# Products of the identity set between a mixer's narrow products, and one run of narrow products cut in two

## The chip, the core and the metric

The kernel runs on one core of one Trainium2 chip. The metric is the device time of one launch, in microseconds (us). Three runs of the kernel before took 1149.23, 1156.27 and 1161.38 us; their median is 1156.27 us.

## What is computed

Two layers, each on 256 tokens of width 1024, then one last RMS norm. A layer is a SwiGLU feed-forward block, a mixer, and a second feed-forward block, each added to the residual with a gate, each on an RMS norm that is scaled and shifted by nine vectors from a conditioning vector. The mixer projects its input once and feeds three branches:

- attention: an indexer of 8 heads of 32 scores every key for every query, the 64 best keys of a query are kept, and 8 heads of 64 attend to these alone (one key and value head is shared by all);
- a state-space mixer: 16 groups of 16 channels with a complex state of 64, written here in chunks of 8 tokens (32 chunks), so that the input of a group's state is one product with a 128 x 128 matrix `R`;
- a convolution of 31 taps with a layer norm and a product.

The three are normalised, joined, and multiplied by `w_out`. All is float32. In the wide products a float32 operand is split into a high and a low part (`hi`, `lo`), and three products of these (helper `mm3`, lines 328 to 330) give the result.

## The kernel before, in words

**Tiling.** Tokens are two tiles of 128 (`t` = 0, 1). The weights come from HBM in units of 128 x 1024, in the order in which they are used; `Stream.prep_one` (lines 100 and 102) splits each unit on ScalarE and VectorE. The feed-forward blocks and the mixer's projections and `w_out` are made of wide products: a moving operand of 256 to 512 columns against 128 rows.

**The mixer** (`mixer`) has eight generators: `W` the projection (one step is 24 wide products, tiles `ps_inB`, `ps_inQ`), `K` the keys, `I` and `J` the indexer for tile 0 and 1 (`att_index`, tile `ps_idx`, line 1201), `S` the state-space branch (`ssm_thread`), `C` the convolution, `a` and `b` the attention for tile 0 and 1 (`att_main`). A string, `MIX_ORDER`, lists whose step is traced next. Around the change it reads `... I W I S J S I W I J J I S W ...`; the third `S` is the run of 16 products `R` x `U` into `ps_V` (line 1301), each 32 columns wide, then two copies to ScalarE's tile `Vs` (1303, 1304).

**The narrow products.** An indexer step makes two products of 32 rows and 128 columns (tile 0) or 256 columns (tile 1). In `att_main`, tile 0 has two banks of four heads and tile 1 four banks of two heads; each head has three products into `ps_lg`: the mask in bfloat16 through the identity `identb` (line 1247), then the high and the low part of the keys (1249, 1250), 128 or 256 columns wide. Then the probabilities are transposed, four 128-column transposes to a bank `ps_PT` (1265), two banks for tile 0 and four for tile 1, and multiplied with the values, 64 columns wide, into `ps_o` (1270).

**What sets the order.** Each engine works its queue in order. The order in a queue is made when the kernel is built: the framework's planner plays the program on a timeline of its own and takes, of the instructions that are ready there, the one traced first. `tc.issue_after(x)` puts the instructions of its block behind `x` on `x`'s engine, with no wait. So a product traced early can come late in the queue, and products of different steps are mixed.

**PSUM.** `ps_idx`, `ps_lg` and `ps_PT` take the banks `a2` and `a3` in turn (two of the `ps_lg` take another pool), `ps_U`, `ps_V` and `ps_Y` the bank `a0`. A product with `start=True` begins its columns anew: what stood there is gone.

Of the kernel before, what the change touches and what calls it, by code (L numbers as in the profile page):

```python
# [17 lines left out]
P = 128  # L18
# [21 lines left out]
NCH = 32  # L40
# [3 lines left out]


MIX_ORDER = """
W K S K K W K J I J J I W I S J S I W I J J I S W I J I J S W C C C I J J I S W
I J I J S I J S W W C C S W a b S N a C a C S S b b a C a b C b a a b b b C b b
b
"""  # L50
# [81 lines left out]
def kernel(  # L132
# [8 lines left out]
    nc = tc.nc  # L141
# [19 lines left out]
    def s1(shape, dtype, nm, tg="a"):  # L161
        return two_p.tile(shape, dtype, tag="s1" + tg, name=nm, bufs=S1B[tg])

    def s2(shape, nm, tg="a", dtype=F32):
        return two_p.tile(shape, dtype, tag="s2" + tg, name=nm, bufs=S2B[tg])

    def b8(shape, nm):
        return two_p.tile(shape, F32, tag="b8", name=nm, bufs=2)

    def bank(pool, nm):  # L170
        return pool.tile([P, 512], F32, tag="b", name=nm)

    def abank(i, nm):
        return ps_a.tile([P, 512], F32, tag=f"a{i}", name=nm)


    ident = const.tile([P, P], F32, name="ident")
    make_identity(nc, ident)
    identb = const.tile([P, P], BF16, name="identb")
    nc.gpsimd.tensor_copy(identb, ident)  # L180
    ones = const.tile([P, 32], F32, name="ones")
    nc.gpsimd.memset(ones, 1.0)
    dmask = ident[:, 112:128]
# [911 lines left out]
    def mixer(l, finish):  # L1095
# [7 lines left out]
        kTl = one_p.tile([P, 256], F32R, tag="kTl", name="kTl")  # L1103
        kiT = one_p.tile([P, 256], F32, tag="kiT", name="kiT")
        qiT = s2([P, 512], "qiT")
# [8 lines left out]
        def merge(t, piece, k0, nk):  # L1114

            pt = bank(ps_m, "ps_mg")
            for k in range(nk):
                nc.tensor.transpose(pt[:, P * k:P * k + P], piece[:, P * k:P * k + P], ident)
            for k in range(nk):
                merged(t, k0 + k, pt[:, P * k:P * k + P], xTh[t][:, k0 + k, :], xTl[t][:, k0 + k, :])  # L1120
# [73 lines left out]
        def att_index(t):  # L1194
            nk = P * (t + 1)
            idx = s1([P, 256], F32, "idx")
            for b in range(4):

                ps = abank(2 + b % 2, "ps_idx")
                for i in range(2):  # L1200
                    nc.tensor.matmul(ps[:, nk * i:nk * i + nk], qiT[32 * b:32 * b + 32, 256 * i + P * t:256 * i + P * t + P],  # L1201
                                     kiT[32 * b:32 * b + 32, :nk], start=True, stop=True)
                rl = s2([P, 512], "rl")
                nc.scalar.activation(rl[:, :2 * nk], ps[:, :2 * nk], AF.Relu, scale=32 ** -0.5)
                for i in range(2):
                    h = b + 4 * i
                    if h == 0:
                        nc.vector.tensor_scalar_mul(idx[:, :nk], rl[:, :nk], wis[:, t, 0:1])
                    else:
                        nc.vector.scalar_tensor_tensor(idx[:, :nk], rl[:, nk * i:nk * i + nk], wis[:, t, h:h + 1],  # L1210
                                                       idx[:, :nk], op0=ALU.mult, op1=ALU.add)
                yield
            nc.vector.memset(idx[0:64, nk - 64:nk], NEG_INADM)
            for r in range(8):
                m8 = sm_p.tile([P, 8], F32, tag="m8", name="m8")
                nc.vector.max(m8, idx[:, :nk])
                nc.vector.match_replace(idx[:, :nk], m8, idx[:, :nk], NEG_TAKEN)
                yield
            mb = s1([P, 256], BF16, "maskb")
            nc.vector.tensor_scalar(mb[:, :nk], idx[:, :nk], NEG_CUT, MASK_BIAS, op0=ALU.is_gt, op1=ALU.mult)  # L1220
            maskb[t] = mb
            yield

        def att_main(t):
            nk = P * (t + 1)
            hpb = 512 // nk
            nb = 8 // hpb

            qT = [s2([P, 512], f"qT{e}", "a", F32R) for e in range(2)]
            for j in range(2):  # L1230
                src = pin["Q"][j].rearrange("p (k n) -> p k n", k=2)[:, :, P * t:P * t + P]
                for e in range(2):
                    r, o = slice(64 * e, 64 * e + 64), slice(64 - 64 * e, P - 64 * e)
                    d = qT[e].rearrange("p (k j n) -> p k j n", k=2, j=2)[:, :, j]
                    nc.scalar.activation(d[r], src[r], AF.Copy)
                    nc.vector.tensor_sub(d[o], src[r], d[r].bitcast(F32))
            yield
            Pm = b8([P, 8, 256], "Pm")
            sums = sm_p.tile([P, 8], F32, tag="sums", name="sums")
            mx = sm_p.tile([P, 8], F32, tag="mx", name="mx")  # L1240
            nmx = sm_p.tile([P, 8], F32, tag="nmx", name="nmx")
            for b in range(nb):
                ps = bank(ps_g, "ps_lg") if t == 1 and b < 2 else abank(2 + b % 2, "ps_lg")
                hb = [2 * (hpb * (b // 2) + i) + b % 2 for i in range(hpb)]
                for i, h in enumerate(hb):
                    r = 64 * (h % 2)
                    nc.tensor.matmul(ps[:, nk * i:nk * i + nk], identb, maskb[t][:, :nk], start=True, stop=False)
                    qh = qT[h % 2][:, P * (h // 2):P * (h // 2) + P]
                    nc.tensor.matmul(ps[:, nk * i:nk * i + nk], qh, kTh[:, :nk], start=False, stop=False)
                    nc.tensor.matmul(ps[:, nk * i:nk * i + nk], qh[r:r + 64], kTl[r:r + 64, :nk], start=False, stop=True)  # L1250
                hs = slice(hb[0], hb[-1] + 1, 2)
                nc.vector.tensor_reduce(mx[:, hs], ps.rearrange("p (h n) -> p h n", h=hpb), axis=mybir.AxisListType.X, op=ALU.max)
                nc.vector.tensor_scalar_mul(nmx[:, hs], mx[:, hs], -0.125)
                for i, h in enumerate(hb):
                    nc.scalar.activation(Pm[:, h, :nk], ps[:, nk * i:nk * i + nk], AF.Exp, bias=nmx[:, h:h + 1],
                                         scale=0.125, accum_out=sums[:, h:h + 1])
                yield
            rin = sm_p.tile([P, 8], F32, tag="rin", name="rin")
            nc.vector.reciprocal(rin, sums)
            po = bank(ps_g, "ps_o")  # L1260
            for b in range(nb):
                pt = abank(2 + b % 2, "ps_PT")
                for i in range(4):
                    h, kt = (4 * b + i, 0) if t == 0 else (2 * b + i // 2, i % 2)
                    nc.tensor.transpose(pt[:, P * i:P * i + P], Pm[:, h, P * kt:P * kt + P], ident)
                PT = s2([P, 512], "PT")
                nc.scalar.activation(PT, pt, AF.Copy)
                for i in range(4):
                    h, kt = (4 * b + i, 0) if t == 0 else (2 * b + i // 2, i % 2)
                    nc.tensor.matmul(po[:, 64 * h:64 * h + 64], PT[:, P * i:P * i + P], vsb[:, kt, :],  # L1270
                                     start=(kt == 0), stop=(kt == t))
                yield
            o = s2([P, 512], "osb")
            nc.vector.tensor_mul(o.rearrange("p (h n) -> p h n", h=8), po.rearrange("p (h n) -> p h n", h=8),
                                 rin.rearrange("p (h o) -> p h o", o=1).to_broadcast([P, 8, 64]))
            rs = rms_col([o], 512)
            nc.vector.tensor_scalar_mul(o, o, rs)
            yield
            merge(t, o, 0, 4)
            yield  # L1280

        def ssm_thread():
            R, O, Tp, Ec, Es, D8 = (SS[n] for n in ("R", "O", "Tp", "Ec", "Es", "D8"))
# [9 lines left out]
            ps = abank(0, "ps_U")  # L1293
            for g in range(G):
                nc.tensor.transpose(ps[:, NCH * g:NCH * g + NCH], Ug[:, g].rearrange("c a j -> c (a j)"), ident[32:32 + NCH, 32:32 + NCH])
            U = s2([P, G, NCH], "U", "s")
            nc.scalar.activation(U.rearrange("p g n -> p (g n)"), ps, AF.Copy)
            yield
            psv = abank(0, "ps_V")
            for g in range(G):  # L1300
                nc.tensor.matmul(psv[:, NCH * g:NCH * g + NCH], R[:, g, :], U[:, g, :], start=True, stop=True)
            Vs = s2([P, 512], "Vs", "s")
            nc.scalar.activation(Vs[0:64, :], psv[64:128, :], AF.Copy)
            nc.scalar.activation(Vs[64:128, :], psv[0:64, :], AF.Copy)
# [23 lines left out]
            for g4 in range(4):  # L1328
                for gq in range(4):
                    g = 4 * gq + g4  # L1330
                    o_ = py[32 * gq:32 * gq + 32, P * g4:P * g4 + P]
                    nc.tensor.matmul(o_, U[:, g, :], Tp[:, :, g, :], start=True, stop=False, tile_position=(0, 32 * gq))
                for gq in range(4):
                    g = 4 * gq + g4
# [17 lines left out]
            pt = bank(ps_m, "ps_yT")  # L1352
# [8 lines left out]
            for q in range(4):  # L1361
                w_ = wg[q // 2]
                cs = slice(512 * (q % 2), 512 * (q % 2) + 512)
                for e in range(2):
                    r, qs = slice(64 * e, 64 * e + 64), slice(P * q, P * q + P)
# [15 lines left out]
            pt = bank(ps_m, "ps_sg")  # L1381
# [200 lines left out]
```

## Time and profile before

| | us |
|---|---|
| profiled execution, its own time | 1159.37 |
| its span on the core | 1157.5 |
| median of the three runs | 1156.27 |
| TensorE busy | 1082.1 (93%) |
| VectorE busy | 881.8 (76%) |
| ScalarE busy | 557.9 (48%) |
| mean granted TensorE clock | 0.954 of full |

The span goes from the first to the last instruction; the profiled execution took 1.9 us more than that. PE is TensorE's matmuls, PEld its weight loads, DVE VectorE, ACT ScalarE, POOL GpSimd, SP the queue of most loads. The granted clock of a stretch is 1.00 at 2.4 GHz and 0.50 at 1.2 GHz. Busy time of PE counts an instruction from its start to its modelled end, so two products in a row overlap in it; the distance from one start to the next is what one costs. In the trace a float32 product that is not split stands as two matmuls.

### The profile page before, as it was taken

Reading aid. Unit: us, or ns where it says so; the run is one execution under the profiler, and the core shown is the slowest. Engines: PE = TensorE matmul, PEld = TensorE weight load, DVE = VectorE, ACT = ScalarE, POOL = GpSimd, SP = SyncE. Lnnn points to the kernel's source line nnn. Section 1 sums busy time; section 2 is a strip of 40 time slices with the busy share of each in tenths; the row PEclk is TensorE's granted clock in tenths of the full one; section 3 lists DMA queues with packets and bytes.
Section 4 is the critical chain, followed back from the end, with each engine's and each line's share of the span. In section 5 each row is a group of like instructions: output and inputs, shape, how many; then the busy total and the mean of one; then the engine's idle time right before and its main releaser. Section 6 shows DMA issues by size and latency. Waiting matters only on the chain.

```text
span 1157.5 us, 19306 instructions
## 1 busy us (share of the span) xinstructions
PE 1082.1 (93%) x7043; PEld 936.8 (81%) x7043; DVE 881.8 (76%) x1791; ACT 557.9 (48%) x979; POOL 93.2 (8%) x176
## 2 busy tenths in 40 slices
PE   5999978998999999999998999999899998999996
PEld 3578867886886878888996799999698687999996
DVE  4479998888597687899856889889678777665655
ACT  4354433446436565563534534444464656444442
POOL 6000101021012000000020000100100000000000
PEclk9899999989797899999999999999999899999998
DMA  9889788996653139768873799999665234767651
GB/s 254 268 268 304 227 258 287 328 292 175 159 149 78 57 103 301 246 223 287 262 220 108 250 323 360 339 317 328 184 165 148 73 91 146 256 210 221 210 160 55
DMA packets 182671, 251.43 MB, mean 217 GB/s; under 512 B 20023, under 2 KB 132865, under 8 KB 182577
## 3 DMA queue, kind: packets, MB, share of 16 engines
q1 hardware_dynamic: 173728, 240.56, 65.3%
q0 software_dynamic: 5792, 7.52, 2.8%
q10 hardware_dynamic: 3056, 2.13, 0.9%
q8 instruction: 55, 0.90, 0.3%
q14 instruction: 40, 0.32, 0.1%
HBM read 245.19 MB, written 1.11 MB: 213 GB/s over the span
## 4 chain that ended last, share of the span: by engine, by line
PE 56%; DMA 7%; DVE 6%; ACT 3%; issue 2%; SPq 1%; ACTq 0%; DVEq 0%
PE ps_gt L328 7%; PE ps_gt L329 7%; PE ps_gt L330 7%; PE ps_y L330 5%; PE ps_y L328 5%; PE ps_y L329 5%; DMA raw<-in_mod_w_dram 3%; DMA raw<-in_ffn_w_gu_dram 2%; DVE lo L102 2%; DVE macc L365 2%; ACT hi L100 1%; PE ps_idx L1201 1%; PE ps_gu L328 1%; PE ps_gu L330 1%; PE ps_cv L1408 1%
## 5 line engine op out<-in xcount | busy, mean ns | idle before, releaser
L100 ACT ACTIVATE hi<-raw 128x1024 fp32r<-128x1024 f32 (+1 forms) x314 | 328.0, 1054 | 315.0 <-DMA raw<-in_ffn_w_gu_dram 105.5
L102 DVE TENSOR_TENSOR lo<-raw,hi 128x1024 fp32r<-128x1024 f32 (+1 forms) x314 | 379.1, 1214 | 121.6 <-ACT hi L100 117.6
L328 PE MATMUL ps_gt<-xTh,hi 128*128 128x256 f32 x1120 | 320.2, 288 | 10.4 <-DVE h L745 6.6
L330 PE MATMUL ps_gt<-xTh,lo 128*128 128x256 f32 x1120 | 314.8, 285 | 4.4 <-DVE lo L102 4.4
L329 PE MATMUL ps_gt<-xTl,hi 128*128 128x256 f32 x1120 | 317.7, 285 | 0.0
L328 PEld LDWEIGHTS ps_gt<-xTh,hi 128*128 128x128 f32 x1120 | 216.2, 193 | 17.4 <-DVE h L745 7.6
L330 PEld LDWEIGHTS ps_gt<-xTh,lo 128*128 128x128 f32 x1120 | 214.4, 193 | 6.2 <-DVE lo L102 5.7
L329 PEld LDWEIGHTS ps_gt<-xTl,hi 128*128 128x128 f32 x1120 | 216.7, 193 | 1.8 <-issue 0.8
L365 DVE SCALAR_TENSOR_TENSOR macc<-raw,cond,macc 128x512 f32<-128x512 f32 x224 | 166.3, 749 | 25.8 <-DMA raw<-in_mod_w_dram 24.3
L329 PE MATMUL ps_y<-lo,hTh 128*128 128x512 f32 x352 | 139.9, 397 | 1.5 <-DVE lo L102 1.5
L330 PE MATMUL ps_y<-hi,hTl 128*128 128x512 f32 x352 | 139.5, 396 | 1.0 <-DVE hTl L749 1.0
L328 PE MATMUL ps_y<-hi,hTh 128*128 128x512 f32 x352 | 133.6, 396 | 4.9 <-ACT hi L100 4.5
L397 POOL DMA_DIRECT2D spill<-mrow x64 | 31.3, 496 | 642.0 <-ACT mrow L394 640.5
L328 PEld LDWEIGHTS ps_y<-hi,hTh 128*128 128x128 f32 x352 | 66.0, 189 | 19.3 <-ACT hi L100 5.3
L330 PEld LDWEIGHTS ps_y<-hi,hTl 128*128 128x128 f32 x352 | 67.1, 191 | 17.1 <-DVE hTl L749 2.1
L329 PEld LDWEIGHTS ps_y<-lo,hTh 128*128 128x128 f32 x352 | 67.3, 191 | 16.3 <-DVE lo L102 3.6
L328 PE MATMUL ps_gu<-hi,xTh 128*128 128x512 f32 x96 | 39.8, 415 | 6.8 <-DVE xTh L324 6.8
L743 ACT ACTIVATE silu<-ps_gt 128x256 f32<-128x256 f32 x70 | 25.3, 378 | 40.8 <-PE ps_gt L330 40.7
L330 PE MATMUL ps_gu<-hi,xTl 128*128 128x512 f32 x96 | 39.7, 414 | 3.0 <-DVE xTl L325 3.0
L329 PE MATMUL ps_gu<-lo,xTh 128*128 128x512 f32 x96 | 38.6, 402 | 0.0
L745 DVE TENSOR_TENSOR h<-silu,ps_gt 128x256 f32<-128x256 f32 x70 | 28.0, 417 | 10.6 <-ACT silu L743 10.4
L748 ACT ACTIVATE hTh<-h 128x256 fp32r<-128x256 f32 x70 | 27.4, 410 | 16.6 <-DVE h L745 15.5
(386 smaller groups left out, 1591.5 us busy)
## 6 DMA issues: line engine op xcount, KB each, us to landing
raw<-in_ffn_w_gu_dram SPq DMA_DIRECT2D x140, 512.0 KB
raw<-in_mod_w_dram SPq DMA_DIRECT2D x128, 512.0 KB
raw<-in_ffn_w_down_dram SPq DMA_DIRECT2D x88, 512.0 KB
raw<-in_ffn_w_gu_dram SPq DMA_DIRECT2D x72, 256.0 KB
raw<-in_w_in_dram SPq DMA_DIRECT2D x20, 512.0 KB
raw<-in_mod_w_dram SPq DMA_DIRECT2D x32, 256.0 KB
raw<-in_w_out_dram SPq DMA_DIRECT2D x16, 512.0 KB
row<-spill POOLq DMA_DIRECT2D x6, 512.0 KB, 4.9
```

Source lines behind the costliest of these rows:

```text
L100: nc.scalar.activation(hi[:, :n], raw[:, :n], AF.Copy)
L102: nc.vector.tensor_sub(lo[:, :n], raw[:, :n], hi[:, :n].bitcast(F32))
L328: return [nc.tensor.matmul(ps, xh, wh, start=start, stop=False), nc.tensor.matmul(ps, xh, wl, start=False, stop=False), nc.tensor.matmul(p ...
L329: nc.tensor.matmul(ps, xh, wl, start=False, stop=False),
L330: nc.tensor.matmul(ps, xl, wh, start=False, stop=stop)]
L365: nc.vector.scalar_tensor_tensor(acc, raw[:, 512 * i:512 * i + 512], cond[:, k:k + 1], prev, op0=ALU.mult, op1=ALU.add)
L397: nc.gpsimd.dma_start(d[:, 256 * q:256 * q + 256], r[32 * q:32 * q + 1, 0:256])
L743: nc.scalar.activation(s, ps[i][:, :256], AF.Silu)
L745: nc.vector.tensor_mul(h, s, ps[i][:, 256:])
L748: nc.scalar.activation(hi, h, AF.Copy)
L1201: nc.tensor.matmul(ps[:, nk * i:nk * i + nk], qiT[32 * b:32 * b + 32, 256 * i + P * t:256 * i + P * t + P], kiT[32 * b:32 * b + 32, :nk], ...
L1408: nc.tensor.matmul(pc[32 * q:32 * q + 32, 256 * ct:256 * ct + 256], SS["W4"][:, 32 * ct + 8 * q + b, :], U4[:, q, ct, b:b + 256], start=(b ...
```

## The change

A helper `fill(ps, c, behind)` makes one bfloat16 product of the identity with copies of itself, 512 - c columns wide, into the columns from `c` to the end of the bank `ps`, behind the product `behind`. Nothing reads what it writes: the products that follow in that bank begin their columns anew.

- In `att_index` one fill of 256 columns stands behind the first product of each bank.
- In `att_main` fills of 384 and 256 columns stand behind the first and second head of each bank of tile 0, and one of 256 columns behind the first head of each bank of tile 1; fills of 384 and 256 columns stand behind the first and second transpose of each bank `ps_PT`.
- In `ssm_thread` fills of 384, 256 and 128 columns stand behind the products 3, 7 and 11. Behind product 7 the step ends, so the 16 products are two steps of 8. `MIX_ORDER` has one `S` more: the second eight, and the two copies, are traced behind a step `W`.

```diff
-W K S K K W K J I J J I W I S J S I W I J J I S W I J I J S W C C C I J J I S W
+W K S K K W K J I J J I W I S J S I W S I J J I S W I J I J S W C C C I J J I S W
...
+    def fill(ps, c, behind):
+
+
+        n = (512 - c) // P
+        with tc.issue_after(behind.ins):
+            nc.tensor.matmul(ps[:, c:].rearrange("p (a n) -> p a n", a=n), identb,
+                             identb.rearrange("p (o n) -> p o n", o=1).to_broadcast([P, n, P]), start=True, stop=True)
...
                 for i in range(2):
-                    nc.tensor.matmul(ps[:, nk * i:nk * i + nk], qiT[32 * b:32 * b + 32, 256 * i + P * t:256 * i + P * t + P],
-                                     kiT[32 * b:32 * b + 32, :nk], start=True, stop=True)
+                    m_ = nc.tensor.matmul(ps[:, nk * i:nk * i + nk], qiT[32 * b:32 * b + 32, 256 * i + P * t:256 * i + P * t + P],
+                                          kiT[32 * b:32 * b + 32, :nk], start=True, stop=True)
+                    if i == 0:
+                        fill(ps, 256, m_)
...
-                    nc.tensor.matmul(ps[:, nk * i:nk * i + nk], qh[r:r + 64], kTl[r:r + 64, :nk], start=False, stop=True)
+                    m_ = nc.tensor.matmul(ps[:, nk * i:nk * i + nk], qh[r:r + 64], kTl[r:r + 64, :nk], start=False, stop=True)
+                    if i < hpb - 1 and i < 2:
+                        fill(ps, nk * i + nk, m_)
...
-                    nc.tensor.transpose(pt[:, P * i:P * i + P], Pm[:, h, P * kt:P * kt + P], ident)
+                    m_ = nc.tensor.transpose(pt[:, P * i:P * i + P], Pm[:, h, P * kt:P * kt + P], ident)
+                    if i < 2:
+                        fill(pt, P * i + P, m_)
...
-                nc.tensor.matmul(psv[:, NCH * g:NCH * g + NCH], R[:, g, :], U[:, g, :], start=True, stop=True)
+                m_ = nc.tensor.matmul(psv[:, NCH * g:NCH * g + NCH], R[:, g, :], U[:, g, :], start=True, stop=True)
+                if g % 4 == 3 and g < 12:
+                    fill(psv, NCH * g + NCH, m_)
+                if g == 7:
+                    yield
```

## Rows read from the trace of the kernel before

**Rows 1.** The page: busy time by engine; the clock in 40 slices; ScalarE's weight splits
```profile
PE 1082.1 (93%) x7043; PEld 936.8 (81%) x7043; DVE 881.8 (76%) x1791; ACT 557.9 (48%) x979; POOL 93.2 (8%) x176
...
PEclk9899999989797899999999999999999899999998
...
L100 ACT ACTIVATE hi<-raw 128x1024 fp32r<-128x1024 f32 (+1 forms) x314 | 328.0, 1054 | 315.0 <-DMA raw<-in_ffn_w_gu_dram 105.5
```

**Rows 2.** The page: the chain that ended last, shares by engine
```profile
PE 56%; DMA 7%; DVE 6%; ACT 3%; issue 2%; SPq 1%; ACTq 0%; DVEq 0%
```

**Rows 3.** Busy time by stretch: length, PE, PEld, DVE, ACT, POOL; clock, DMA; layer 0
```profile
301.10:321.60 20.50, 20.50 (x83) 18.01 (x84) 10.01 (x18) 6.12 (x10) 0.13 (x1) 0.50 0.32 90
...
362.50:383.00 20.50, 18.87 (x71) 14.41 (x71) 13.20 (x55) 11.80 (x45) 0.55 (x1) 0.50 0.10 29
```

**Rows 4.** The same view, layer 1
```profile
855.70:864.30 8.60, 8.60 (x65) 7.56 (x64) 4.55 (x10) 3.30 (x7) 0.00 (x0) 1.00 0.74 207
864.30:867.70 3.40, 3.40 (x17) 3.18 (x16) 3.14 (x7) 1.55 (x3) 0.00 (x0) 0.50 0.02 5
...
908.70:918.90 10.20, 9.43 (x36) 6.83 (x35) 8.70 (x37) 6.76 (x30) 0.55 (x1) 0.50 0.16 52
918.90:954.00 35.10, 34.89 (x194) 28.70 (x194) 25.72 (x86) 22.49 (x57) 0.00 (x0) 1.00 0.29 89
```

**Rows 5.** Timeline of PE, layer 0: start, us, line, count, idle before
```profile
301.06 2.08 PE L1201 MATMUL ps_idx<-kiT,qiT 32*128 32x256 f32 x8 [0.65 <-ACT qiT L1191]
...
308.20 5.33 PE L1301 MATMUL ps_V<-U,sl_R 128*128 128x32 f32 x24
...
329.73 0.43 PE L1332 MATMUL ps_Y<-sl_Tp,U 128*32 128x128 f32 x8
```

**Rows 6.** Timeline of PE, layer 1, the same steps
```profile
855.74 1.14 PE L1201 MATMUL ps_idx<-kiT,qiT 32*128 32x256 f32 x8
...
859.66 2.87 PE L1301 MATMUL ps_V<-U,sl_R 128*128 128x32 f32 x24
...
864.60 0.58 PE L328 MATMUL ps_inB<-xTh,hi 128*128 128x256 f32 x1
...
876.59 0.43 PE L1332 MATMUL ps_Y<-sl_Tp,U 128*32 128x128 f32 x8
```

**Rows 7.** Timeline of PE at the start of attention, layer 0 and layer 1
```profile
351.49 0.48 PE L1366 MATMUL ps_glu<-hi,yT 128*128 128x512 f32 x1
...
898.03 0.23 PE L1247 MATMUL ps_lg<-maskb,identb 128*128 128x128 bf16 x1
...
898.35 0.48 PE L1366 MATMUL ps_glu<-hi,yT 128*128 128x512 f32 x1
```

**Rows 8.** Tile ps_y from 380 and from 920 us: ns min/median/max, first and last start
```profile
L328 PE MATMUL ps_y<-hi,xTh x32: 389/389/497, 383.3 to 412.6; 128*128 128x512 f32 x32
...
L328 PE MATMUL ps_y<-hi,xTh x32: 389/390/501, 926.9 to 953.8; 128*128 128x512 f32 x32
```

**Rows 9.** Lines by shape, from 351.0, 908.7 and 918.9 us: busy, mean ns, idle
```profile
L1247 PE MATMUL ps_lg<-maskb,identb 128*128 128x128 bf16 x8 | 1.8, 229 | 0.0
...
L1247 PE MATMUL ps_lg<-maskb,identb 128*128 128x256 bf16 x4 | 1.6, 395 | 0.8 <-DVE qT L1236 0.8
...
L1247 PE MATMUL ps_lg<-maskb,identb 128*128 128x256 bf16 x4 | 1.1, 278 | 0.0
```

**Rows 10.** Timeline of PE: the mask's products at half and at full clock
```profile
909.20 0.29 PE L1247 MATMUL ps_lg<-maskb,identb 128*128 128x128 bf16 x1
...
919.21 0.27 PE L1247 MATMUL ps_lg<-maskb,identb 128*128 128x256 bf16 x1
919.24 0.36 PE L1249 MATMUL ps_lg<-kTh,qT 128*128 128x256 f32 x1
```

**Rows 11.** Timeline of VectorE, layer 1: end of the state-space inputs, the mask
```profile
871.69 0.67 DVE L1325 TENSOR_TENSOR X<-X,z 128x496 f32<-128x496 f32 x1
...
892.97 0.22 DVE L1220 TENSOR_SCALAR maskb<-idx 128x128 bf16<-128x128 f32 x1
```

## The prediction

> **What bounds the kernel now.** I read the page first: TensorE is busy 93% of the span and the next engine 76% [rows 1], and TensorE alone is 56% of the chain that ended last [rows 2]. So a microsecond of TensorE's queue is, to first order, a microsecond of time. The page's line of the granted clock then shows where this engine is slowed: the lowest digits lie in the first mixer (the 7s), with an 8 in the second [rows 1]. The change touches the mixers alone, so I went on with busy time by stretch, cut where the clock changes. Four stretches of the mixers run at 0.50 of the clock, that is at 1.2 GHz: 20.5 and 20.5 us in layer 0 [rows 3], 3.4 and 10.2 us in layer 1 [rows 4], 54.6 us in all. In the first and third of them TensorE never waits; in the other two it waits 1.6 and 0.8 us (length less PE busy). The reader is to see that the clock was lost while the engine had work all the time: in layer 1 it was busy 8.60 of 8.60 us before the fall at 864.3 [rows 4], and what it did there was narrow, 24 records of 32 columns in 2.87 us among others [rows 6]. After the fall it ran wide products from 864.60 and had its clock back at 867.7 [rows 4, 6]. In layer 0 the same 24 records took 5.33 us [rows 5].
>
> **What a microsecond at half clock costs.** The two layers run the same instructions, so they price it. From the indexer's first products to the first `ps_Y`, layer 0 takes 329.73 - 301.06 = 28.67 us with 20.5 us at half clock, layer 1 876.59 - 855.74 = 20.85 us with 3.4 us [rows 3 to 6]. The difference, 7.82 us over 17.1, is 0.46 us for each. From the first `ps_glu` to the last start of a `w_out` product layer 0 takes 412.6 - 351.49 = 61.1 us and layer 1 953.8 - 898.35 = 55.5 us, with 20.5 and 10.2 us at half clock [rows 3, 4, 7, 8]: 0.54 for each, more than halving a clock can cost, because layer 0 also waits more. I take 0.46 throughout.
>
> **The change part by part.**
>
> *The fills' own cost.* A layer gets 8 fills in the indexer (8 x 256 = 2,048 columns), 4 and 4 in the logits (2 x 640 + 4 x 256 = 2,304), 12 among the transposes (6 x 640 = 3,840) and 3 among the state-space inputs (768): 31 fills, 8,960 columns; 62 and 17,920 in both. The nearest row is the mask, which is also a bfloat16 product with the identity as weights. At full clock 128 columns take 229 ns and 256 take 278 ns [rows 9], so a column is 49/128 = 0.38 ns; at half clock 290 and 395 ns [rows 9, 10], 0.82 ns. That is 6.9 us if all run at full clock and 14.7 us if all run at half. The low end is the distance of starts: behind a mask of 256 columns the next product begins 0.03 us later [rows 10], since its weights load meanwhile; 62 x 0.03 is 2 us. I take the column price, because a fill is followed by narrow products that leave little to hide it under, with a quarter of the fills at half clock: 6.9 + 0.25 x 7.8 = **+8.9 us**.
>
> *The clock.* What is bought is the 54.6 us. From above it is worth 54.6 x 0.46 = 25 us, from below nothing. I take a part, place by place. In layer 0 the first fall comes at 301.1, as the indexer begins, behind 0.65 us of idle for ScalarE [rows 5]; no fill stands before that point, so it stays. The return should come earlier, because wide products now run between the two halves of the 16: 7 of 20.5 us. In layer 1 the run of narrow products in front of 864.3 is cut in two and partly filled; it should lose its clock about every third time instead of always, 1 to 2 us of 3.4, so I count 1. In attention the logits of tile 0 are filled most thinly, four fills to 24 products, and right behind them TensorE waits for the queries (0.8 us of idle [rows 9]); I expect the fall to stay. But the transposes that follow get 640 columns to every four, and there I expect it back: 9 of 20.5 us in layer 0, 4.5 of 10.2 in layer 1. Sum: 21.5 us fewer at half clock, 21.5 x 0.46 = **-9.9 us**.
>
> A rule of the Trainium skill speaks against this term. Rows 4 show a clock lost with no idle at all. The page "TensorE: Matmul & The Clock Gate", section "Why this matters for your kernels", puts drops in the middle of a kernel down to idle gaps between bursts of matmuls. By that rule fills between products that already follow each other buy nothing, and the sum would be the fills' cost alone; the trace at 864.3 disagrees, so I keep the term, and the rule comes back as a rival.
>
> *The second eight behind a step `W`.* No product is added or lost, only the order changes: the last 8 products, the two copies to `Vs` and what hangs on them come behind as many as 24 wide products. On TensorE that is nothing. Ahead of the copies stands one weight split more on ScalarE, 1.05 us [rows 1], on an engine that is busy 3.3 of 8.6 us there [rows 4]: hidden. Who waits is the state-space chain, which ends with `X` at 872.4 and feeds `ps_Y` at 876.6 [rows 6, 11]: 4.2 us of room. A split that puts 12 to 24 wide products between the halves uses about 1.4 to 2.9 us of it at full clock (3.4 us at half clock held 17 starts [rows 4], 0.2 us each, so 0.1 to 0.12 at full). Zero; if the whole move falls into half clock, 24 x 0.2 = 4.8 us and 0.6 us are left uncovered. The step's loads from HBM keep their number and order on SP's queue, and POOL's queue is not passed.
>
> *VectorE as the next bound.* The top-k rounds end with the mask at 893.2 and its first product starts at 898.0 [rows 7, 11]: 4.8 us of room in layer 1. They hang on the indexer, which moves forward with TensorE. Zero.
>
> *The planner.* Longer steps shift its timeline and may reorder products near the waits. The two attention stretches at half clock hold 2.4 us of waits; I allow 3 us either way and take zero.
>
> *Sum.* +8.9 - 9.9 = -1.0 us. The profiled execution took 1159.4 us, so this gives 1158.4; it lies 3.1 us above the median of the runs shown, so for a median I say **1155 us**. The case as such spans 1148 to 1162 (fills 2 to 14.7 us less the clock's part, plus the planner).
>
> **Rivals.**
>
> *The clock is held throughout.* Then all 54.6 us go: -25 + 6.9 = -18 us, 1138 us. For it: layer 1 kept its clock in places where layer 0 lost it, so the margin is thin. Against: the fall at 301.1 has no fill ahead of it, and the logits of tile 0 get less fill than the transposes. It decides itself at the first `ps_lg`: if the clock is 1.00 through them in both layers, this is the case. Chance 0.16.
>
> *Fills buy nothing.* The clock falls in the same places for as long, and the fills run inside those stretches. In layer 0 both stretches are at half clock nearly throughout, 8,960 x 0.82 = 7.3 us; in layer 1 about half, 5.4 us. +12.7 us: 1156.3 + 12.7 = 1169 us, or 1163 with all at 0.38 ns. Slower than before. Its place is the logits and the transposes, and the point is whether more than three of the four stretches keep their length. For it: at half clock a narrow stretch has twice as long to stay narrow, as the 20.5 us show. Against: behind a run of wide products the clock was back at 867.7 [rows 4, 6], and fills are as wide. This is what the skill's rule on idle gaps, named above, would come to. Chance 0.19.
>
> *The split does not split.* If the wide products of that step are placed elsewhere by the planner, the two eights run one after the other, and the state-space part of the gain, 8 x 0.46 = 3.7 us, is lost: 1159 us. Against: in layer 1 the wide products at 864.60 stand right behind the narrow run, so they are at hand. Chance 0.13.
>
> **How the numbers follow.** The forecast has 0.52, the rivals 0.16, 0.19 and 0.13. Within 1%, some 11.6 us, is about what a measurement of this kernel can tell from no change: the runs before spread over 12 us. Faster by over 1% (under 1144.7) is most of the first rival and a little of the forecast: 0.15. Slower by over 1% (over 1167.8) is half of the second rival and the edge of the others: 0.12. The rest, 0.73, is no change. The range that leaves out 2 in 10 goes from 1142, inside the first rival, to 1167, inside the second.
>
> **What would show it.** In the profile after, 31 more bfloat16 matmuls per mixer, with start-to-start costs of some 0.1 to 0.16 us; `ps_V` in two groups with `ps_inB` between; the stretches at 0.50 in the mixers 33 us in sum instead of 54.6, the longest of them shorter than 20.5; the fall at the logits still there, and the clock back while the transposes run. Wrong would be: no stretch at 0.50 left at the logits (first rival), or over 45 us still there (second). Waits of TensorE for `X`, or for the mask, would show that the order cost something.

## The result, and the profile after

Four runs of the changed kernel took 1161.89 to 1172.93 us, median 1167.43, beside 1158.83 for four runs of the kernel before. The comparison gives a ratio of 1.0139 with a 95% interval of [1.0093, 1.0184]. Twelve more runs, told of below, gave 1.0094 [1.0058, 1.0130]. These ratios leave out a kernel's slow runs, those over 1.5% above its fastest; over all runs the medians of the four are 0.7% apart, and so are the means of the twelve and their 35 of the kernel before. So the change made the kernel slower, by 0.7 to 1.4%. The forecast was 1155 us, no change.

The profiled execution took 1162.93 us (span 1161.1), against 1159.37 (span 1157.5). Its page, the lines that answer to [rows 1, 2] (busy time, clock in 40 slices, chain of waits):

```profile
PE 1090.1 (94%) x7105; PEld 937.9 (81%) x7105; DVE 881.4 (76%) x1791; ACT 558.3 (48%) x979; POOL 93.1 (8%) x176
...
PEclk9999989989897999999999999999959899999998
...
PE 60%; DVE 14%; DMA 13%; issue 6%; ACT 6%; SPq 1%; POOL 0%; ACTq 0%; DVEq 0%; POOLq 0%
```

TensorE has 62 instructions more (7105 against 7043) and is still the engine that bounds; the others do what they did. One of the two 7s of the first mixer is an 8 now, but the second mixer has a 5. Busy time by stretch, cut where the clock is 0.50 inside the mixers, answers to [rows 3, 4] and has their columns:

```profile
308.20:315.00 6.80, 6.80 (x25) 4.83 (x25) 4.26 (x9) 2.04 (x4) 0.00 (x0) 0.50 0.24 77
349.10:366.20 17.10, 17.10 (x60) 11.79 (x60) 11.08 (x39) 10.11 (x40) 0.95 (x2) 0.50 0.26 78
844.10:871.40 27.30, 27.30 (x106) 21.20 (x105) 9.97 (x21) 6.73 (x11) 0.00 (x0) 0.50 0.23 70
912.30:919.10 6.80, 6.80 (x24) 4.59 (x25) 5.62 (x28) 5.26 (x25) 0.00 (x0) 0.50 0.22 72
```

Three stretches are shorter than before (20.5, 20.5 and 10.2 us), as the change meant, and one is far longer: 27.3 us where 3.4 stood. Together they are 58.0 us, against 54.6. TensorE was busy in all of them to the last hundredth. This is one execution; a second one of the same kernel, shown further down, has other stretches. The long one begins inside the indexer. TensorE's timeline there, layer 1 (it answers to [rows 6]):

```profile
842.70 0.69 PE L1210 MATMUL ps_idx<-kiT,qiT 32*128 32x256 f32 x2 [0.97 <-ACT qiT L1200]
843.32 0.28 PE L187 MATMUL ps_idx<-identb 128*128 128x256 bf16 x1
843.53 0.75 PE L1210 MATMUL ps_idx<-kiT,qiT 32*128 32x256 f32 x4
844.22 0.40 PE L187 MATMUL ps_idx<-identb 128*128 128x256 bf16 x1
844.54 1.21 PE L1210 MATMUL ps_idx<-kiT,qiT 32*128 32x256 f32 x2
845.69 0.58 PE L337 MATMUL ps_inB<-xTh,hi 128*128 128x256 f32 x1
...
852.18 1.75 PE L1316 MATMUL ps_V<-U,sl_R 128*128 128x32 f32 x8
853.75 0.40 PE L187 MATMUL ps_V<-identb 128*128 128x256 bf16 x1
853.80 0.56 PE L337 MATMUL ps_inB<-xTh,hi 128*128 128x256 f32 x1
...
861.12 1.75 PE L1316 MATMUL ps_V<-U,sl_R 128*128 128x32 f32 x8
```

Before, the two indexer steps were one row of 8 records, 1.07 us from their first start to the next product's (855.74 [rows 6] to 856.81). TensorE's timeline of the kernel before goes on so:

```profile
856.81 0.39 PE L328 MATMUL ps_inB<-xTh,hi 128*128 128x256 f32 x1
...
859.02 0.71 PE L1201 MATMUL ps_idx<-kiT,qiT 32*128 32x128 f32 x4
```

Now the same 8 records and two fills take 842.70 to 845.69, 2.99 us, the last 1.6 of them after the clock's fall at 844.1. From 852.18 the reader sees that the split did split: wide `ps_inB` products stand between the two halves of the 16 products (a row of 8 records is four products).

**Work and loss.** The clock falls in other places in every execution, so single profiles don't compare well: the loss defined here ranged from 39 to 65 us over 35 runs of the kernel before. Each run lists its span and its mean granted clock. Their product I call the work, the time that the span would have taken at full clock; the rest of the span is the loss. For the changed kernel (12 runs) and the kernel before (35) on one chip: work 1110.9 against 1099.4, **+11.5 ± 0.8 us**; loss 50.9 against 53.9, **-2.9 ± 1.7 us** (± is one standard error, here and below). The change costs more work than forecast and buys less clock. The two are not quite independent: over the runs of the kernel before on each chip, work falls by 0.2 to 0.3 us for each microsecond of loss.

### The profile page after: what moved, and what is told of

Read it like the earlier page. It is cut to its first block, busy times and chain, and to the rows that moved or that the text cites. A ratio compares the mean times of both kernels' runs of the same rounds, so it can differ in the third digit from the quotient of the medians.

```text
span 1161.1 us, 19439 instructions
## 1 busy us (share of the span) xinstructions
PE 1090.1 (94%) x7105; PEld 937.9 (81%) x7105; DVE 881.4 (76%) x1791; ACT 558.3 (48%) x979; POOL 93.1 (8%) x176
## 4 chain that ended last, share of the span: by engine, by line
PE 60%; DVE 14%; DMA 13%; issue 6%; ACT 6%; SPq 1%; POOL 0%; ACTq 0%; DVEq 0%; POOLq 0%
PE ps_gt L337 7%; PE ps_gt L339 7%; PE ps_gt L338 7%; PE ps_y L339 5%; PE ps_y L337 5%; PE ps_y L338 5%; DVE lo L102 5%; DMA raw<-in_mod_w_dram 5%; DMA raw<-in_ffn_w_gu_dram 5%; DVE macc L374 4%; ACT hi L100 2%; PE ps_idx L1210 2%; ACT hf L330 1%; PE ps_cv L1427 1%; DMA raw<-in_ffn_w_down_dram 1%
## 5 line engine op out<-in xcount | busy, mean ns | idle before, releaser
L374 DVE SCALAR_TENSOR_TENSOR macc<-raw,cond,bias 128x512 f32<-128x512 f32 x32 | 24.0, 749 | 15.5 <-DMA raw<-in_mod_w_dram 12.7
L757 ACT ACTIVATE hTh<-h 128x256 fp32r<-128x256 f32 x70 | 27.4, 409 | 17.1 <-DVE h L754 16.1
```

The lines of the kernel that those rows point to most:

```text
L374: nc.vector.scalar_tensor_tensor(acc, raw[:, 512 * i:512 * i + 512], cond[:, k:k + 1], prev, op0=ALU.mult, op1=ALU.add)
L757: nc.scalar.activation(hi, h, AF.Copy)
```

## The experiments

All are single parts or variants of the change, each run 12 times (the indexer's part alone 6 times). Three theories stood at the start, named in the expectations: (A) that the fills cost the time themselves, as work that the clock does not pay back; (B) that the new order does, the extra `S` and the split; and (C) that the indexer's fills part steps that used to run side by side. The experiments came in three series, each on a chip of its own with 29 to 35 runs of the kernel before. The table has differences in work and loss to these, over all runs; the ratio is that of the comparison. In the cuts of code only the lines in question stand.

| kernel | ratio [95%] | work, us | loss, us |
|---|---|---|---|
| split only | 1.0003 [0.9964, 1.0041] | -0.3 ± 1.1 | -1.6 ± 2.2 |
| state-space part (split, its 6 fills) | 1.0008 [0.9970, 1.0045] | -1.7 ± 1.0 | -1.0 ± 2.2 |
| indexer's 16 fills | 1.0107 [1.0043, 1.0170] | +4.9 ± 1.6 | +4.2 ± 1.7 |
| attention's 40 fills | 1.0038 [0.9994, 1.0082] | +6.1 ± 1.3 | -5.3 ± 2.2 |
| logits' 16 fills | 1.0035 [1.0001, 1.0069] | +5.2 ± 1.1 | -0.5 ± 1.6 |
| transposes' 24 fills | 1.0029 [0.9988, 1.0070] | +3.3 ± 1.2 | -1.9 ± 2.1 |
| transposes' fills, state-space part | 1.0020 [0.9977, 1.0064] | +4.5 ± 1.2 | -0.3 ± 2.5 |
| all but the indexer's fills | 0.9940 [0.9906, 0.9973] | +7.1 ± 1.1 | -9.4 ± 2.9 |
| indexer's fills on 32 rows | 0.9984 [0.9950, 1.0018] | +0.5 ± 0.7 | -3.7 ± 2.2 |
| indexer's fills ahead of the pair | 1.0008 [0.9969, 1.0046] | -0.2 ± 0.8 | +0.6 ± 1.9 |
| the whole change | 1.0094 [1.0058, 1.0130] | +11.5 ± 0.8 | -2.9 ± 1.7 |
| the change, indexer's fills on 32 rows | 0.9951 [0.9915, 0.9986] | +6.9 ± 1.2 | -9.3 ± 2.7 |

**Which part costs it.** First the four parts, each alone.

*Split only*: the `S` more and the `yield` behind product 7, no fill.

```diff
...
-                if g % 4 == 3 and g < 12:
-                    fill(psv, NCH * g + NCH, m_)
                 if g == 7:
                     yield
...
```

> The sixteen state-space products in two steps of eight with the extra step S, and no fill at all. Work is span times mean granted clock (1104.7 us in the profile before, 1112.3 after), loss is span minus work (52.8 and 48.8 us). Theory A (the fills are work that the clock does not pay back): work within 1.5 us of before, loss as before, time within 0.5% of before. Theory B (the new order is what costs, because it cuts the wide products into runs too short to bring the clock back, as in the 27 us at half clock of layer 1 after the change): work as before, loss up by 8 us or more, time +0.7% or more. Theory C (the fills part indexer products that used to run side by side): nothing here.

1154.29 us, ratio 1.0003, no work and no loss to tell from zero. That the order does it, theory B, falls.

*State-space part*: the same with its six fills.

```diff
...
+                if g % 4 == 3 and g < 12:
+                    fill(psv, NCH * g + NCH, m_)
                 if g == 7:
                     yield
...
```

> The state-space part of the change whole: two steps of eight, the extra step S, and its 6 fills (1,536 columns). Theory A: work +0.6 to +1 us, loss as before, time within 0.5% of before. Theory B: loss up by 8 us or more, as in the run without fills, and time +0.7% or more. If the fills help where they stand, loss is 3 us or more under that of the run with the split alone.

1151.95 us, 1.0008: neither cost nor gain.

*Attention's fills*: those of the logits and of the transposes, with the old order.

```diff
...
+                    if i < hpb - 1 and i < 2:
+                        fill(ps, nk * i + nk, m_)
...
+                    if i < 2:
+                        fill(pt, P * i + P, m_)
...
```

> Only the 40 fills of attention (16 among the logits, 24 among the transposes, 12,288 columns); state-space products and indexer as before. Theory A: work +4 to +6 us (12,288 columns at 0.38 ns are 4.7 us), loss within 5 us of before, time +0.3% to +0.6%. Theory B: no order is changed, so time as before or better. Theory C: nothing here beyond theory A. If the fills do hold the clock in attention, loss falls by 8 us or more.

1154.85 us, 1.0038. They cost 6.1 us of work and give 5.3 of loss back, about even.

*Indexer's fills*: these 16 alone.

```diff
...
+                    if i == 0:
+                        fill(ps, 256, m_)
...
```

> Only the 16 fills of the indexer (4,096 columns); everything else as before. Theory A by columns alone: work +1.6 us. Theory C (two indexer steps on different 32 rows no longer overlap once a product of 128 rows stands between): work +3 to +5 us, the eight records at the start of the indexer no longer within 1.1 us at full clock but over 2 us without the fills' own time. Loss within 5 us of before in both. Theory B: as before.

1164.50 us, 1.0107: 16 fills of 256 columns alone make the kernel as slow as the whole change does. They add 4.9 us of work, 0.31 us a fill, and the loss grows too. TensorE's timeline of this kernel, at full clock but for the row at 298.22 and the end of the last, shows why:

```profile
295.90 0.69 PE L1210 MATMUL ps_idx<-kiT,qiT 32*128 32x256 f32 x2 [0.52 <-ACT qiT L1200]
296.53 0.28 PE L187 MATMUL ps_idx<-identb 128*128 128x256 bf16 x1
296.74 0.70 PE L1210 MATMUL ps_idx<-kiT,qiT 32*128 32x256 f32 x4
297.38 0.28 PE L187 MATMUL ps_idx<-identb 128*128 128x256 bf16 x1
297.59 0.70 PE L1210 MATMUL ps_idx<-kiT,qiT 32*128 32x256 f32 x2
298.22 0.58 PE L337 MATMUL ps_inB<-xTh,hi 128*128 128x256 f32 x1
...
301.92 0.48 PE L1210 MATMUL ps_idx<-kiT,qiT 32*128 32x128 f32 x2
302.34 0.28 PE L187 MATMUL ps_idx<-identb 128*128 128x256 bf16 x1
302.55 0.48 PE L1210 MATMUL ps_idx<-kiT,qiT 32*128 32x128 f32 x2
302.96 3.52 PE L1312 MATMUL ps_V<-U,sl_R 128*128 128x32 f32 x24
```

The pair of steps takes 295.90 to 298.22, 2.32 us instead of 1.07; the step of 128 columns 1.04 us instead of 0.64 (859.02 to 859.66 before). The fill itself holds only 0.21 us, from its start to the next. The rest is what it parts. Two steps use different 32-row quarters of the array, and without a fill their products run side by side. The product on all 128 rows starts 0.63 us behind the first one of the step, when that one is nearly through, and the next step's start only behind it. Theory C expected over 2 us for the pair without the fills' own time; it is 1.90. Only two of a layer's eight steps ran side by side before; the other six stood alone, and a step of 128 columns pays 0.40 us, half of it for the fill itself.

**Is it the parting or the time?** Two kernels have the same 16 fills, with nothing parted.

*On 32 rows*: the fill uses only the rows that its step uses.

```diff
...
-                        fill(ps, 256, m_)
+                        fill(ps, 256, m_, slice(32 * b, 32 * b + 32))
...
```

> Only the indexer's 16 fills, at the same places and of the same 256 columns, but each on the 32 rows of its own step instead of all 128. Theory C (a product of 128 rows between the two products of a step parts it from the step beside it, which uses 32 other rows): the steps overlap again, so work is +0 to +2 us instead of the +4.8 us of 128 rows (1103.7 against 1098.9), and time within 0.4% of before. If instead each fill costs its 0.2 to 0.3 us whatever its rows are, work is +4 to +5 us again.

1154.01 us, 0.9984; work +0.5 ± 0.7. The same columns in the same places cost next to nothing once the rows fit.

*Ahead of the pair*: two fills on all rows, traced ahead of every second step.

```diff
...
+                if b % 2 == 0:
+                    for _ in range(2):
+                        fill(ps, 256, None)
...
```

> Only the indexer's fills, 16 of 256 columns on 128 rows as in the change, but two at once ahead of every second step, so that none stands inside a step or inside a pair of steps. Theory C: the pair runs side by side behind them, work +2 to +3 us (a fill's own 0.1 to 0.2 us at full clock, sixteen times), against +4.8 inside the steps; loss as before (55 us) or less, against 59.3. If the columns themselves cost it, work is +4.8 again.

1158.27 us, 1.0008; work -0.2 ± 0.8, where one theory (C) expected 2 to 3 us. The timeline shows that in each layer the planner put the first two long before their pair, which ran as one row of 8 again. The other twelve stand where they were meant, right ahead of a step or a pair.

```profile
270.82 0.38 PE L187 MATMUL ps_idx<-identb 128*128 128x256 bf16 x2 [0.34 <-DVE ytmp L345]
...
297.48 1.14 PE L1213 MATMUL ps_idx<-kiT,qiT 32*128 32x256 f32 x8
298.55 0.39 PE L337 MATMUL ps_inB<-xTh,hi 128*128 128x256 f32 x1
...
311.47 0.39 PE L187 MATMUL ps_idx<-identb 128*128 128x256 bf16 x2
311.79 1.14 PE L1213 MATMUL ps_idx<-kiT,qiT 32*128 32x128 f32 x8
```

Two such fills hold 0.32 us (311.47 to 311.79), and behind them the eight records, a step of each tile, run side by side in 1.07 us (to 312.86). That no work shows is not the fills' price alone: in this order three pairs of steps a layer run side by side, before only one, which gives some of it back. What the two make apart was not measured.

**The change less its bad part.** *All but the indexer's fills*:

```diff
...
-                    if i == 0:
-                        fill(ps, 256, m_)
...
```

> The whole change without the indexer's 16 fills. If those fills are what made the change slower: time within 0.5% of before (the parts measured alone add to +6.0 - 1.7 = +4 us of work and -5.3 - 1.0 = -6 us of loss, so 1154 us against 1156). If the parts do not add, and the change has a cost as a whole, it stays 0.7% or more slower.

1153.16 us, 0.9940 [0.9906, 0.9973]. Without these 16 fills the loss is 9.4 us under that of the kernel before, and the kernel is no longer slower.

*Logits' fills only*:

```diff
...
+                    if i < hpb - 1 and i < 2:
+                        fill(ps, nk * i + nk, m_)
...
```

> Only the 16 fills among the logits (4,608 columns); none among the transposes. The 40 fills of attention gave work +6.0 and loss -5.3 us. If the logits' fills are what keeps the clock up, loss stays 4 to 6 us under before with work at +2 to +2.5 us, and time falls by 2 to 4 us (0.2% to 0.3%). If the transposes' fills bring the clock back earlier, as the prediction had it, loss is as before here and time +0.2%.

1161.90 us, 1.0035: 5.2 us of work and no clock bought. Here the row of the fill does not explain the price:

```profile
913.63 0.38 PE L1259 MATMUL ps_lg<-kTl,qT 64*128 64x256 f32 x1
913.95 0.28 PE L187 MATMUL ps_lg<-identb 128*128 128x256 bf16 x1
914.07 0.27 PE L1256 MATMUL ps_lg<-maskb,identb 128*128 128x256 bf16 x1
```

0.12 us from its start to the next, within the prediction's "some 0.1 to 0.16 us", and between a 64-row and a 128-row product, which were parted before as well. Sixteen of these are 2 us; some 3 us of the 5.2 I could not place. They may in part be chance: attention's fills less the transposes' alone, 6.1 - 3.3, make 2.8 ± 1.8 us for the logits'.

**The mended change.** The last series has the whole change again, the change with 32-row fills in the indexer, and the transposes' fills alone and with the state-space part.

*The whole change*, unchanged:

> The change as it is, in more runs, beside the three below. Work +10 to +13 us over before (the parts measured alone: indexer +4.8, attention +6.0, state space -1.7; the four runs of the result 1112.2 against 1099), loss within 3 us of before, time +0.6% to +1.2%.

1164.03 us, 1.0094 [1.0058, 1.0130].

*With 32-row fills in the indexer*:

```diff
...
-                        fill(ps, 256, m_)
+                        fill(ps, 256, m_, slice(32 * b, 32 * b + 32))
...
```

> The change with one thing mended: the indexer's 16 fills on the 32 rows of their step. If the parting of side-by-side steps is what made the change slower, work is 4 to 6 us under the change as it is, and time at or under before (0.993 to 1.000 of it), as without these fills (0.994). If the fills cost it in another way once all stand together, it stays at +0.6% or more.

1152.77 us, 0.9951 [0.9915, 0.9986] to the kernel before: the whole change's 62 fills with 16 of them on fewer rows, and 11.0 ± 2.0 us less than the whole change (means 1152.7 and 1163.7). Work fell by 4.6 us, loss by 6.4. Its timeline at the first pair:

```profile
296.01 0.80 PE L1210 MATMUL ps_idx<-kiT,qiT 32*128 32x256 f32 x3 [0.37 <-ACT qiT L1200]
296.55 0.27 PE L187 MATMUL ps_idx<-identb 32*128 32x256 bf16 x1
296.66 0.38 PE L1210 MATMUL ps_idx<-kiT,qiT 32*128 32x256 f32 x2
296.88 0.27 PE L187 MATMUL ps_idx<-identb 32*128 32x256 bf16 x1
296.88 0.70 PE L1210 MATMUL ps_idx<-kiT,qiT 32*128 32x256 f32 x3
297.51 0.39 PE L337 MATMUL ps_inB<-xTh,hi 128*128 128x256 f32 x1
```

1.50 us for the pair, and fills start at the same instant as products of the next step (296.88 twice). Its stretches at half clock in the mixers are 27.2 us in sum, all that there are:

```profile
344.00:361.00 17.00, 17.00 (x60) 11.77 (x60) 11.01 (x39) 10.06 (x38) 0.90 (x2) 0.50 0.25 78
849.20:852.60 3.40, 3.40 (x15) 2.75 (x14) 3.24 (x6) 1.11 (x3) 0.00 (x0) 0.50 0.51 154
893.50:900.30 6.80, 6.80 (x27) 4.88 (x26) 5.90 (x32) 5.96 (x27) 0.00 (x0) 0.50 0.12 40
```

That execution, 1142.88 us, was the fastest of its twelve, so it shows where the clock can be held, not how often. How sure the gain is: over all runs the means are 1152.7 and 1155.2 us, 2.5 ± 2.0 apart. That it beats the change is clear of the noise; that it beats the kernel before rests on the comparison above, whose interval ends at 0.9986.

*Transposes' fills only*, and *with the state-space part*:

```diff
...
+                    if i < 2:
+                        fill(pt, P * i + P, m_)
...
```

> Only the 24 fills among the transposes (7,680 columns). From attention whole (work +6.0, loss -5.3) less the logits alone (work +5.2, loss about 0): work +1 to +3 us, loss -4 to -6 us, time -0.2% to -0.4%. If attention's gain needs both, loss is as before and time +0.1% to +0.3%.

> The fills among the transposes and the whole state-space part; none in the indexer and none among the logits. If the logits' fills only cost: work +0 to +2 us, loss -5 to -8 us, time -0.4% to -0.7%, at or under the change without the indexer's fills (0.994). If they are needed: above 0.996.

1157.28 us, 1.0029, and 1157.03 us, 1.0020: no gain. By the mark set beforehand (above 0.996) the logits' fills are needed: the parts that gain nothing alone gain together with them (loss -9.4 ± 2.9 against -0.3 ± 2.5 without). Whether that is so, or the sum of errors of 2 to 3 us each, these runs don't settle.

## Why the prediction was wrong

**The bound was right.** TensorE bounds before and after, and the work that was added to its queue came out as time. By definition work and loss add up to the span: +11.5 - 2.9 = +8.6 us, beside 8.5 by the times.

**Two terms of the sum failed, by about 5 us each, and the indexer's 16 fills are behind both.** The fills' cost, "I take the column price", was too small (11.5 us of work where 6.9 were priced at full clock), and the clock's gain was forecast too large (7.9 us by the count used here, 2.9 measured). The whole change with only these 16 fills on fewer rows has 4.6 ± 1.2 us less work and 6.4 ± 2.7 us less loss, together 11.0 ± 2.0; the forecast of -1.0 us missed the measured 8.5 by 9.5.

**The first step: the fills' own cost.** At 0.38 ns a column the 17,920 columns are 6.9 us of full-clock time; measured as work they were 11.5 ± 0.8. By place, priced against measured alone: transposes 2.9 and 3.3 ± 1.2, right; state-space 0.6 and -1.7 ± 1.0 with the split; logits 1.8 and 5.2 ± 1.1; indexer 1.6 and 4.9 ± 1.6. The indexer's error is shown to its cause: the sum of all `ps_idx` groups of layer 1, first start to the next product, half-clock stretches halved, is 5.7 us before, 8.0 with the fills on 128 rows and 5.6 on 32 rows (with both kinds of fills three pairs of steps stand next to each other, before only one), so 2 x 2.3 = 4.6 us for both layers. The row to see it by was there: 8 records in 1.14 us beside 4 records of the same shape in 1.13 (862.45, before) say that the second step was free, and a price per column of the product put between does not hold what it parts. The Trainium skill has this in the page "TensorEngine Tiling (Array Packing)", section "Key Properties": a change of tiling mode drains TensorE. The trace agrees: a 128-row fill starts 0.63 us behind the product in front of it and holds 0.21 us, where one among the logits holds 0.12. I had weighed the clock rule and not this one.

**The second step: the clock, place by place.** The term was forecast at -9.9 us, or -7.9 with the fills that run at half clock counted here; measured -2.9 ± 1.7. By place, the profile after seems to bear most of it out: layer 0 at the indexer 6.8 us at half clock for 20.5 (13.7 gained, forecast 7), attention 17.1 for 20.5 and 6.8 for 10.2 (3.4 each, forecast 9 and 4.5), 20.5 us in sum where 20.5 were forecast for these three, and all undone by 27.3 us in the fourth, where "I count 1" was written. That agreement is luck. The second execution of the same kernel, the profile of "the whole change" (1169.78 us), gained nothing in the three places and has as much in the fourth, there from 847.5, three microseconds before the first `ps_idx`:

```profile
297.90:308.10 10.20, 10.20 (x46) 9.24 (x45) 2.82 (x6) 1.93 (x3) 0.00 (x0) 0.50 0.34 113
311.60:321.80 10.20, 10.20 (x41) 8.01 (x41) 6.47 (x12) 2.20 (x5) 0.13 (x1) 0.50 0.16 51
352.50:373.00 20.50, 20.50 (x62) 12.69 (x62) 12.30 (x43) 10.97 (x39) 3.43 (x5) 0.50 0.30 93
847.50:857.70 10.20, 10.20 (x43) 7.51 (x42) 5.07 (x8) 4.04 (x7) 0.00 (x0) 0.50 0.45 129
861.10:878.20 17.10, 17.10 (x66) 12.72 (x65) 7.26 (x14) 4.20 (x7) 0.00 (x0) 0.50 0.15 56
915.70:925.90 10.20, 10.20 (x36) 6.91 (x37) 8.73 (x35) 6.21 (x29) 0.00 (x0) 0.50 0.19 60
```

Fourteen executions were profiled in all, one of each kernel and a second of the changed one. Their time at half clock, by layer, tells more. From the first `ps_idx` to the first `ps_Y` it is 18.3 ± 3.0 us where fills on 128 rows stand between the indexer's products (6 layers) and 8.7 ± 1.4 where none does (22). From the first `ps_lg` or `ps_glu` product to the last start of a `w_out` product it is 14.0 ± 1.8 where the logits' and the transposes' fills both stand (10 layers) and 19.3 ± 2.2 where neither does (12; layers taken as independent). So for both layers attention's forecast of -13.5 us at half clock came out as -11 ± 6, about right, while the fills at the indexer, where -8 was forecast, cost 19 ± 7 us more. That the fills there lose clock, the runs show; how they do it stays open. Parting is not needed for a long stretch: with the transposes' fills alone, and the indexer as it was, layer 1 has one of 20.5 us:

```profile
845.10:865.60 20.50, 20.50 (x83) 17.98 (x84) 10.02 (x18) 6.12 (x10) 0.13 (x1) 0.50 0.27 83
```

**What would show it.** The fall at the logits stayed, as said, though in layer 0 it came ahead of most of them, at 349.1, among `ps_glu` products; and the clock came back while the transposes ran (366.2, 919.1). The fall at 301.1, said to stay, is not in the profile after, whose first pair of the indexer ran at full clock. The first rival's test, no half clock at the logits, did not come. The second's, over 45 us, did (58.0), and its time (1169 or 1163) is the nearest, but its reason is not what happened on the whole: the fills bought clock in attention, and those of the indexer lost it. The third rival, a split that does not split, is out by the rows at 852.18 to 861.12.

**The rule of the Trainium skill on idle gaps**, from "TensorE: Matmul & The Clock Gate", section "Why this matters for your kernels", came near in time for the wrong reason as well. The fall at 844.1 does not speak against it, for 0.97 us of idle stand 1.4 us in front of it. The fall at 349.1 does: TensorE was busy in 14.10 of the 14.10 us before, so there the trace disagrees, as it did at 864.3.

**Terms put at zero.** The second eight behind a step `W` is zero as said (1.0003). TensorE's waits in the profile after, from 842 to 960 us, name neither `X` nor the mask.

## What to carry to other kernels

Before a product is put between two others, see whether these run side by side: where a row's time for 8 is that of 4, they do, and a product on more rows between them costs what it parts, here three times the price of its columns. Give filler work the rows of its neighbours. And where a throttle moves from run to run, split every run into work (span times granted clock) and loss: over twelve runs the work is known to about 1 us here, while times of one kernel lie up to 30 us apart. For the same reason one profile does not say where a change gained clock.

## What the runs showed of the chip

- Two indexer steps on different 32-row quarters take 1.07 us [rows 6]; one step alone takes 1.06, by TensorE's timeline of the kernel before. The second costs nothing.

```profile
862.45 1.13 PE L1201 MATMUL ps_idx<-kiT,qiT 32*128 32x256 f32 x4
863.51 0.41 PE L1301 MATMUL ps_V<-U,sl_R 128*128 128x32 f32 x2
```

- The clock fell in the middle of two-part products 128 and 64 rows high that followed each other without a gap. TensorE's timeline of the changed kernel, layer 0, around the fall at 349.1:

```profile
348.39 0.50 PE L1386 MATMUL ps_glu<-lo,yT 64*128 64x512 f32 x1
348.81 0.54 PE L1385 MATMUL ps_glu<-hi,yT 128*128 128x512 f32 x1
349.29 0.79 PE L1386 MATMUL ps_glu<-lo,yT 64*128 64x512 f32 x1
```

  They are 512 columns wide, and the clock fell all the same. Nothing here says why. Busy time by stretch before the fall:

```profile
335.00:349.10 14.10, 14.10 (x127) 8.66 (x119) 11.08 (x41) 5.69 (x11) 7.81 (x12) 1.00 0.38 106
```

- One kernel's loss to the clock ranged from 39 to 65 us between its runs (35 of the kernel before, one chip), a spread larger than any effect studied here.
